# A hybrid decoder block on one core: expert gate and up weights loaded as two neighbouring rows per partition, and large tiles set at multiples of 128 bytes

## The chip, the core and the metric

The kernel runs on one core of one Trainium2 chip, as a single launch. The metric is the device time of one execution in microseconds (us). Three runs of the kernel before gave 1133.46, 1133.92 and 1135.08 us; their median is 1133.92 us.

The engines are called by the profile's names: PE (matrix multiply; PEld is its weight load), DVE (vector), ACT (scalar), POOL (GpSimd) and SP (here nearly only an issuer of DMAs). A name with a q at its end (SPq, ACTq) is the instruction queue of that engine.

## The reference

512 tokens of width 1024 go through one block: a mixer (retention, differential attention, gates and an output projection w_out) and a mixture of 32 experts. The change touches the second half and the vectors that feed it. All data are float32.

```
h  = rmsnorm(x, norm_ffn) * (1 + sc2) + sh2
gp = softmax(h @ w_router_group + b)          # 4 groups, the best one is taken
el = (h @ w_router_expert + b)                # 8 experts in a group, the best two are taken
y  = (silu(x_e @ w_exp_gate[e]) * (x_e @ w_exp_up[e])) @ w_exp_down[e]    # for each expert e
x  = x + g2 * sum of the two weighted y of each token
```

w_exp_gate and w_exp_up are 1024 x 512 for each expert, w_exp_down is 512 x 1024. Each of the three is 2 MB for one expert, so all 32 experts read 192 MB from memory.

## The kernel before

The trace has four stages: modulation vectors (0 to 95 us), projections, retention and attention (to about 590), w_out with the router for four chunks of 128 tokens (590 to 640), and the experts (640 to 1115), after which the result is normalised and written.

**Split matrices.** w_out is multiplied in high and low parts. A staging tile `wst` of 128 x 4 x 512 is loaded (L171). `split_kp` (L160) lets ACT copy half of it to `whi` (L163), and DVE subtract to get `wlo` (L164). The second column half of w_out has four such pairs; three go this way, the fourth (`hi4`, `lo4`, in the trace `ew`) through ACT at L1071 and POOL at L1072. All four pairs are needed before chunk 0 of the router stage can finish its product with w_out at L209, and the router chunks follow that.

**Router.** `wr` holds the router's weights, 128 partitions x 8 blocks x 36 columns; block k holds channels 128k to 128k+127. ACT's queue issues the two DMAs that fill it (L782, L783), then two for the biases `br`. `router_weights` (L801 to L805, DVE) folds norm and modulation into them. The token chunk `x1` is transposed in blocks of 128 channels (L870), and block k of `wr` meets block k of the transposed chunk in the logits (L877). `rows2` (L626) carries the modulation rows and norm_ffn; one transpose turns it into the columns `sh2` and `A2`, one column for each block of channels.

**Experts.** The work goes in 13 units of PE work of about 32 us each. A unit gathers the tokens of its experts by a product with a 0/1 matrix (L1000), transposes the gathered rows `xs` (L1031, eight transposes of 128 x 128), multiplies by gate and up (L1222), applies silu, multiplies by down (L1242) and adds the result back (L1269, L1275). The order of SP's instructions is the order of the code in `run_experts`: `load_in` issues eight loads for an expert (4 pairs of gate and up, L662), `load_down` four (L670). Each load is 512 KB into one of 36 weight slots of 4096 bytes per partition, used in turn (`wtile`, L643 to L650), so the slots hold three experts. A slot's next load waits until PE has used its last content. Loads for the first four units are of fixed experts, later ones are chosen by numbers that SP reads at run time (`chosen`).

A gate or up load takes rows 128(2kp) to 128(2kp)+255 of the matrix, two blocks, so that a partition gets two runs of 2048 bytes from places 256 KB apart. A down load gives each partition one run of 4096 bytes.

**Semaphores of DMAs.** DMAs issued by SP and ACT share eight completion semaphores, DMAHW0 to DMAHW7, given in turn in program order. An instruction that uses one again waits until the DMA before it on the same semaphore has landed.

**Pools.** SBUF tiles lie in pools that grow from the left or from the right end. Of the weight slots, those in `hp`, `mw1` and `mw4` are on the left and begin at multiples of 128 bytes; the 18 in `mw2` and `mw3` are on the right and begin 96 bytes past one, as do `wst`, `whi` and `wlo`. No code around the router or the experts sets an order by a planner: ACT, POOL and SP run in program order as built by the scheduler, and DVE and PE in an order written by hand for the router (L1073, L1085).

Of the kernel before, what the change touches and what calls it, by code (L numbers as in the profile page):

```python
# [7 lines left out]
F32 = mybir.dt.float32  # L8
# [5 lines left out]
ALU = mybir.AluOpType  # L14
# [32 lines left out]
ROTARY = (0, 0, 1, 1, 1)  # L47
ROWS_AT, COL_AT = 6, 12
LAMBDA_INIT = 0.8 - 0.6
TWO_PI = 2.0 * np.pi  # L50
# [50 lines left out]


class Rows:

# [15 lines left out]
def block_kernel(tc, a, out):  # L120
# [3 lines left out]
    def left(name, bufs=1):  # L124
        return open_pool(tc, name, bufs, side="left", reuse_waits="tile")

    def right(name, bufs=1):
        return open_pool(tc, name, bufs, side="right", reuse_waits="tile")

    w_in = a["w_in"][0]  # L130

    cp, cp_close = left("consts")
    hp, hp_close = left("hT")
    hla, hla_close = left("hla")
# [490 lines left out]

    rows2 = dp.tile([24, P], F32, name="rows2")  # L626
    nc.sync.dma_start(rows2[0:16, :], modrow[1:3, :].rearrange("s (k p) -> (s k) p", p=P))
    nc.sync.dma_start(rows2[16:24, :], a["norm_ffn"].rearrange("o (k p) -> (o k) p", p=P))
    sh2 = small("sh2", KD)
    A2 = small("A2", KD)  # L630
    run(out_steps)
    ps = pm.tile([P, S], F32, name="ps")
    pe.transpose(ps[:, 0:24], rows2, ident[0:24, 0:24])
    vec.tensor_copy(sh2, ps[:, 0:8])
    vec.tensor_scalar(A2, ps[:, 8:16], 1.0, None, op0=ALU.add)
    vec.tensor_mul(A2, A2, ps[:, 16:24])

# [17 lines left out]
    def load_in(srcs):  # L655

        ws = [{} for _ in srcs]
        for kp in range(KD // 2):
            for w, src in zip(ws, srcs):
                for name in ("w_exp_gate", "w_exp_up"):  # L660
                    w[name, kp] = wtile()
                    nc.sync.dma_start(w[name, kp], src(name)[:, 2 * kp:2 * kp + 2, :])  # L662
        return ws
# [9 lines left out]
    def fixed(e):  # L673
        return lambda name: a[name][0, e].rearrange("(k p) n -> p k n", p=P)

    def chosen(reg):
        return lambda name: a[name][0, bass.ds(reg, 1)].rearrange("e (k p) n -> p (e k) n", p=P)

# [84 lines left out]
    xp, xp_close = left("x1")  # L763
    gp, gp_close = left("gather")
    hh2, hh2_close = left("h2")
    rt, rt_close = right("router")
# [14 lines left out]
    nc.scalar.dma_start(g1b, modrow[0].partition_broadcast(P))  # L781
    nc.scalar.dma_start(wr[:, :, 0:4], a["w_router_group"][0].rearrange("(k p) n -> p k n", p=P))  # L782
    nc.scalar.dma_start(wr[:, :, 4:36], a["w_router_expert"][0].rearrange("(k p) n -> p k n", p=P))  # L783
    nc.scalar.dma_start(br[:, 0:4], a["b_router_group"][0].partition_broadcast(P))
# [48 lines left out]
    class Chunk:  # L833
# [30 lines left out]
        def turn(self, g):  # L864
            if g == 0:
                self.xT = rt.tile([P, KD, P], F32, name="x1T", bufs=2)
            ps = pm.tile([P, S], F32, name="ps")
            for q in range(4):
                k = 4 * g + q
                pe.transpose(ps[:, q * P:(q + 1) * P], x1[:, self.i, k * P:(k + 1) * P], ident)  # L870
            act.copy(self.xT[:, 4 * g:4 * g + 4, :], ps.rearrange("p (k t) -> p k t", k=4))
# [92 lines left out]
    class Gather:  # L964
# [60 lines left out]
        def turn(self, xT):  # L1025
            self.xT = xT
            for j in range(2):
                pt = self.pt() if j == 0 else self.pa()
                for q in range(4):
                    k = 4 * j + q  # L1030
                    pe.transpose(pt[:, q * P:(q + 1) * P], self.xs[:, k * P:(k + 1) * P], ident)  # L1031
                for q in range(4):
# [144 lines left out]
    mw3, mw3_close = right("mw3")  # L1177
    mk, mk_close = right("moe")

    places = slots(mw1, 5, 7) + slots(mw2, 10) + slots(mw3, 8) + slots(mw4, NMW4)  # L1180
# [344 lines left out]
    hp_close()  # L1525
    dram_close()
    cp_close()

# [23 lines left out]
```

## Time and profile before

| what | value |
|---|---|
| median of three runs | 1133.92 us |
| the profiled execution | 1135.46 us |
| its span, first to last instruction | 1133.7 us |
| mean granted TensorE clock | 0.989 |
| PE busy | 1071.7 us (95%) |
| PEld busy | 665.0 us (59%) |
| DVE busy | 622.2 us (55%) |
| ACT busy | 338.4 us (30%) |
| POOL busy | 79.0 us (7%) |
| read from memory | 280.88 MB |

The profiled execution took 1.5 us more than the median, of which 1.8 us lie outside the span. PE is busy in nearly every slice of the span, DMA engines are at 90% or more from about 620 us on, and both stay so until 1105 us; the page's busy shares do not tell which of the two sets the time of which stretch, so the queries below look at stretches, at the waits in them and at the rates of single stretches.

### The profile page before, as it was taken

The numbers are of one execution on the slowest core, as the hardware profiler recorded it, in microseconds if no ns is written. First come the engines' busy times: TensorE is split into PE (matmuls) and PEld (weight loads), VectorE is DVE, ScalarE is ACT, GpSimd is POOL, SyncE is SP. The second block draws the span as 40 slices with busy tenths as digits, with TensorE's granted clock in tenths as the row PEclk, the third lists the DMA queues.
The fourth block names the chain that finished last, engine by engine and source line by source line (L and its number), as shares of the span: only waits on it lengthen the run. The fifth ranks groups of instructions, "written<-read, shape, count | busy, mean of one in ns | idle before, by whom it ended". The sixth has DMA issues, their size and how long they took to land.

```text
span 1133.7 us, 15015 instructions
## 1 busy us (share of the span) xinstructions
PE 1071.7 (95%) x5178; PEld 665.0 (59%) x5178; DVE 622.2 (55%) x1443; ACT 338.4 (30%) x701; POOL 79.0 (7%) x106
## 2 busy tenths in 40 slices
PE   5999999999999999999999899999999999999885
PEld 3777778778788776788877444444432443234222
DVE  3468667644445765655775765755442553244244
ACT  4553233333343534444334211111111110111123
POOL 1031000000021111000013100000000000000001
PEclk9999999999999999999999999999999999999998
DMA  9945645622323221244286899999999999999994
GB/s 317 274 149 186 222 132 185 204 76 81 105 82 105 75 74 39 75 151 146 91 278 235 302 373 391 391 400 393 391 392 400 392 391 391 400 393 394 389 397 159
DMA packets 139889, 284.02 MB, mean 251 GB/s; under 512 B 10977, under 2 KB 34585, under 8 KB 139681
## 3 DMA queue, kind: packets, MB, share of 16 engines
q1 hardware_dynamic: 136656, 281.29, 68.6%
q10 hardware_dynamic: 3152, 1.73, 0.6%
q8 instruction: 42, 0.69, 0.3%
q14 instruction: 39, 0.31, 0.1%
HBM read 280.88 MB, written 2.11 MB: 250 GB/s over the span
## 4 chain that ended last, share of the span: by engine, by line
PE 67%; DMA 19%; DVE 7%; ACT 2%; issue 2%; POOL 1%; SPq 0%; ACTq 0%; DVEq 0%; POOLq 0%
PE pj L209 31%; PE gu L1222 12%; DMA ew<-in_w_exp_up_dram 9%; DMA ew<-in_w_exp_down_dram 5%; PE py L1242 5%; PE pa L1000 4%; PE pa L1269 4%; DMA wa<-in_w_ada_dram 3%; PE pj L391 2%; PE ps L485 2%; PE ps L695 1%; DMA wst<-in_w_in_dram 1%; DVE acc L462 1%; PE ps L391 1%; DVE qk L448 1%
## 5 line engine op out<-in xcount | busy, mean ns | idle before, releaser
L1222 PE MATMUL gu<-ew,xT 128*64 128x512 f32 (+1 forms) x1088 | 222.4, 601 | 12.6 <-DMA ew<-in_w_exp_gate_dram 8.4
L209 PE MATMUL pj<-ew,whi 128*128 128x512 f32 x512 | 168.2, 410 | 0.0
L164 DVE TENSOR_TENSOR wlo<-wst,whi 128x1024 fp32r<-128x1024 f32 x79 | 100.0, 1267 | 87.0 <-ACT whi L163 79.5
L209 PE MATMUL pj<-whi,ew 128*128 128x512 f32 x384 | 131.0, 409 | 2.8 <-DVE v L480 2.8
L1222 PEld LDWEIGHTS gu<-ew,xT 128*64 128x64 f32 (+1 forms) x1088 | 54.4, 123 | 133.7 <-issue 88.4
L1242 PE MATMUL py<-ew,hTm 128*64 128x512 f32 (+1 forms) x544 | 116.1, 599 | 6.9 <-DMA ew<-in_w_exp_down_dram 6.8
L163 ACT CAST whi<-wst 128x1024 fp32r<-128x1024 f32 x79 | 82.8, 1050 | 130.3 <-PE pj L209 122.1
L209 PEld LDWEIGHTS pj<-ew,whi 128*128 128x128 f32 x512 | 94.2, 190 | 23.6 <-issue 2.8
L209 PE MATMUL pj<-ew,wlo 128*128 128x512 f32 x256 | 101.8, 398 | 0.0
L209 PEld LDWEIGHTS pj<-whi,ew 128*128 128x128 f32 x384 | 73.6, 192 | 22.8 <-DVE v L480 3.2
L1275 DVE TENSOR_TENSOR x<-x,pa 128x512 f32<-128x512 f32 x96 | 59.5, 682 | 47.4 <-PE pa L1269 47.4
L1247 DVE SCALAR_TENSOR_TENSOR yt<-py,ws,g2b 64x512 f32<-64x512 f32 x52 | 39.0, 750 | 72.3 <-PE py L1242 71.7
L1242 PEld LDWEIGHTS py<-ew,hTm 128*64 128x64 f32 (+1 forms) x544 | 27.9, 123 | 84.1 <-issue 44.3
L209 PE MATMUL pj<-wlo,ew 128*128 128x512 f32 x192 | 76.9, 401 | 0.0
L1227 DVE TENSOR_TENSOR sg<-sg,gu 64x512 f32<-64x512 f32 x26 | 17.9, 690 | 97.1 <-ACT sg L1226 96.3
L209 PEld LDWEIGHTS pj<-ew,wlo 128*128 128x128 f32 x256 | 48.5, 189 | 11.7
L1269 PE MATMUL pa<-xs,ct 128*128 128x512 f32 x196 | 52.8, 409 | 0.1
L209 PE MATMUL pj<-xhi,whi 128*128 128x512 f32 x128 | 51.7, 404 | 0.0
L1269 PEld LDWEIGHTS pa<-xs,ct 128*128 128x128 f32 x196 | 35.0, 188 | 26.9 <-issue 12.4
L209 PE MATMUL pj<-xhi,wlo 128*128 128x512 f32 x128 | 50.7, 396 | 0.0
L209 PE MATMUL pj<-xlo,whi 128*128 128x512 f32 x128 | 50.7, 396 | 0.0
L1263 ACT CAST xs<-yt 128x512 fp32r<-128x512 f32 x25 | 15.5, 619 | 112.9 <-DVE yt L1247 68.1
(364 smaller groups left out, 1548.1 us busy)
## 6 DMA issues: line engine op xcount, KB each, us to landing
ew<-in_w_exp_gate_dram SPq DMA_DIRECT2D x128, 512.0 KB, 10.6
ew<-in_w_exp_up_dram SPq DMA_DIRECT2D x128, 512.0 KB, 10.7
ew<-in_w_exp_down_dram SPq DMA_DIRECT2D x128, 512.0 KB, 10.4
wa<-in_w_ada_dram SPq DMA_DIRECT2D x44, 512.0 KB, 4.8
wst<-in_w_in_dram SPq DMA_DIRECT2D x20, 1024.0 KB, 5.6
wst<-in_w_in_dram SPq DMA_DIRECT2D x16, 512.0 KB, 4.3
wst<-in_w_ret_o_dram SPq DMA_DIRECT2D x4, 1024.0 KB, 4.9
wst<-in_w_diff_o_dram SPq DMA_DIRECT2D x4, 1024.0 KB
```

The costliest lines, as they stand in the source:

```text
L163: act.copy(hi, src[:, off:off + 2, :])
L164: vec.tensor_sub(lo, src[:, off:off + 2, :], hi.bitcast(F32))
L209: pe.matmul(bank, l, r, start=(k == 0 and j == 0), stop=(k == KD - 1 and j == 2))
L391: pe.matmul(bank, w, (hhi, hhi, hlo)[m][:, k, :], start=(k == 0 and m == 0), stop=(k == KD - 1 and m == 2))
L485: pe.matmul(out, l[a_], r[b_], start=start and j == 0, stop=stop and j == 2)
L1000: pe.matmul(ps, self.G[:, i, :], hx[:, i, ns], start=(i == 0 and j == 0), stop=(i == NT - 1 and j == 1))
L1222: pe.matmul(self.gu[r:r + n, :], self.g.xT[:, k, c:c + n], w[name, k // 2][:, k % 2, :], start=(k == 0), stop=(k == KD - 1))
L1227: vec.tensor_mul(self.sg, self.sg, self.gu[64:P, :])
L1242: pe.matmul(py[r:r + n, :], self.hT[:, k, n * q:n * q + n], w[k][:, nh, :], start=(k == 0), stop=(k == 3))
L1247: vec.scalar_tensor_tensor(yt[r, ns], py[64 * nh:64 * nh + 64, :], self.g.w[r], g2b[r, ns], op0=ALU.mult, op1=ALU.mult)
L1269: pe.matmul(po, self.ct[:, i * P:(i + 1) * P], self.ys[nh][:, j, :], start=start and j == 0, stop=(j == 1))
L1275: vec.tensor_add(x1[:, i, ns], x1[:, i, ns], po)
```

## The change

**Pads.** A tile of 24 floats (96 bytes per partition) is taken first from the right end, and another of 8 floats in the pool `moe`. In the pools `gather` and `moe` the large tiles are taken once in a row ahead of the small ones. In the built program all large tiles then begin at multiples of 128 bytes, the 18 right-hand weight slots and `wst`, `whi` and `wlo` among them.

**Gate and up.** A load now takes rows 256q + 2p and 256q + 2p + 1 into partition p: two neighbouring rows, one run of 4096 bytes. The bytes, the slots and the number of loads stay. With that, block k = 2q + j of a matrix holds channels 256q + 2p + j instead of 128k + p.

**What has to match.** A new function `block(x, k)` reads these channels out of a row, that is every second float. It is used in the router's 32 transposes and in the 104 transposes of gathered rows. `rows2` becomes 12 rows of 256, turned by two transposes. `wr` is filled by eight DMAs on ACT's queue (for each of four q the group's and the expert's columns) in place of two; the number of small pieces, 1024 of 16 bytes and 1024 of 128 bytes, is the same.

```diff
--- before.py
+++ after.py
@@ -46,6 +46,8 @@
 START_STEPS = (1, 2, 2, 2, 1)
 ROTARY = (0, 0, 1, 1, 1)
 ROWS_AT, COL_AT = 6, 12
+
+TOP_PAD, MOE_PAD = 24, 8
 LAMBDA_INIT = 0.8 - 0.6
 TWO_PI = 2.0 * np.pi
 
@@ -100,6 +102,11 @@
     return parts
 
 
+def block(x, k):
+
+    return x.rearrange("s (q c j) -> s q j c", j=2, c=P)[:, k // 2, k % 2, :]
+
+
 class Rows:
 
 
@@ -130,6 +137,8 @@
     w_in = a["w_in"][0]
 
     cp, cp_close = left("consts")
+    top, top_close = right("top")
+    top.tile([P, TOP_PAD], F32, name="pad")
     hp, hp_close = left("hT")
     hla, hla_close = left("hla")
     rot, rot_close = left("rotary")
@@ -623,17 +632,20 @@
     mg = [hlb.tile([P, 2, KD, P], F32R, name=f"mg{i}") for i in range(NT)]
 
 
-    rows2 = dp.tile([24, P], F32, name="rows2")
-    nc.sync.dma_start(rows2[0:16, :], modrow[1:3, :].rearrange("s (k p) -> (s k) p", p=P))
-    nc.sync.dma_start(rows2[16:24, :], a["norm_ffn"].rearrange("o (k p) -> (o k) p", p=P))
+    rows2 = dp.tile([12, 2 * P], F32, name="rows2")
+    nc.sync.dma_start(rows2[0:8, :], modrow[1:3, :].rearrange("s (q c) -> (s q) c", c=2 * P))
+    nc.sync.dma_start(rows2[8:12, :], a["norm_ffn"].rearrange("o (q c) -> (o q) c", c=2 * P))
     sh2 = small("sh2", KD)
     A2 = small("A2", KD)
     run(out_steps)
     ps = pm.tile([P, S], F32, name="ps")
-    pe.transpose(ps[:, 0:24], rows2, ident[0:24, 0:24])
-    vec.tensor_copy(sh2, ps[:, 0:8])
-    vec.tensor_scalar(A2, ps[:, 8:16], 1.0, None, op0=ALU.add)
-    vec.tensor_mul(A2, A2, ps[:, 16:24])
+    for j in range(2):
+        pe.transpose(ps[:, 12 * j:12 * j + 12], block(rows2, j), ident[0:12, 0:12])
+    cols2 = ps[:, 0:24].rearrange("p (j s q) -> p j s q", j=2, s=3)
+    sh2v, A2v = [t.rearrange("p (q j) -> p j q", j=2) for t in (sh2, A2)]
+    vec.tensor_copy(sh2v, cols2[:, :, 0, :])
+    vec.tensor_scalar(A2v, cols2[:, :, 1, :], 1.0, None, op0=ALU.add)
+    vec.tensor_mul(A2v, A2v, cols2[:, :, 2, :])
 
 
     def slots(pool_, *places):
@@ -659,7 +671,7 @@
             for w, src in zip(ws, srcs):
                 for name in ("w_exp_gate", "w_exp_up"):
                     w[name, kp] = wtile()
-                    nc.sync.dma_start(w[name, kp], src(name)[:, 2 * kp:2 * kp + 2, :])
+                    nc.sync.dma_start(w[name, kp].rearrange("p j n -> p (j n)"), src(name)[:, kp, :])
         return ws
 
     def load_down(srcs):
@@ -671,10 +683,13 @@
         return ws
 
     def fixed(e):
-        return lambda name: a[name][0, e].rearrange("(k p) n -> p k n", p=P)
+        return lambda name: (a[name][0, e].rearrange("(k p) n -> p k n", p=P) if name == "w_exp_down" else
+                             a[name][0, e].rearrange("(q p j) n -> p q (j n)", p=P, j=2))
 
     def chosen(reg):
-        return lambda name: a[name][0, bass.ds(reg, 1)].rearrange("e (k p) n -> p (e k) n", p=P)
+        at = bass.ds(reg, 1)
+        return lambda name: (a[name][0, at].rearrange("e (k p) n -> p (e k) n", p=P) if name == "w_exp_down" else
+                             a[name][0, at].rearrange("e (q p j) n -> p (e q) (j n)", p=P, j=2))
 
 
     dohi = hla.tile([P, KD, S], F32R, name="xhi")
@@ -762,6 +777,8 @@
 
     xp, xp_close = left("x1")
     gp, gp_close = left("gather")
+    for name, cols in (("G", NT * P), ("xs", D), ("xT", D), ("oht", P)):
+        gp.tile([P, cols], F32, name=name, bufs=1)
     hh2, hh2_close = left("h2")
     rt, rt_close = right("router")
     mw1, mw1_close = left("mw1")
@@ -779,8 +796,11 @@
     wr = rt.tile([P, KD, 36], F32, name="wr")
     br = rt.tile([P, 36], F32, name="br")
     nc.scalar.dma_start(g1b, modrow[0].partition_broadcast(P))
-    nc.scalar.dma_start(wr[:, :, 0:4], a["w_router_group"][0].rearrange("(k p) n -> p k n", p=P))
-    nc.scalar.dma_start(wr[:, :, 4:36], a["w_router_expert"][0].rearrange("(k p) n -> p k n", p=P))
+    wrv = wr.rearrange("p (q j) n -> p q j n", j=2)
+    for q in range(KD // 2):
+        rs = slice(2 * P * q, 2 * P * q + 2 * P)
+        nc.scalar.dma_start(wrv[:, q, :, 0:4], a["w_router_group"][0, rs].rearrange("(p j) n -> p j n", j=2))
+        nc.scalar.dma_start(wrv[:, q, :, 4:36], a["w_router_expert"][0, rs].rearrange("(p j) n -> p j n", j=2))
     nc.scalar.dma_start(br[:, 0:4], a["b_router_group"][0].partition_broadcast(P))
     nc.scalar.dma_start(br[:, 4:36], a["b_router_expert"][0].partition_broadcast(P))
     nc.scalar.dma_start(iota, a["cst"][:, C_IOTA:C_IOTA + 512])
@@ -867,7 +887,7 @@
             ps = pm.tile([P, S], F32, name="ps")
             for q in range(4):
                 k = 4 * g + q
-                pe.transpose(ps[:, q * P:(q + 1) * P], x1[:, self.i, k * P:(k + 1) * P], ident)
+                pe.transpose(ps[:, q * P:(q + 1) * P], block(x1[:, self.i, :], k), ident)
             act.copy(self.xT[:, 4 * g:4 * g + 4, :], ps.rearrange("p (k t) -> p k t", k=4))
 
         def logits(self, g):
@@ -1028,7 +1048,7 @@
                 pt = self.pt() if j == 0 else self.pa()
                 for q in range(4):
                     k = 4 * j + q
-                    pe.transpose(pt[:, q * P:(q + 1) * P], self.xs[:, k * P:(k + 1) * P], ident)
+                    pe.transpose(pt[:, q * P:(q + 1) * P], block(self.xs, k), ident)
                 for q in range(4):
                     k = 4 * j + q
                     if j:
@@ -1176,6 +1196,9 @@
     mw2, mw2_close = right("mw2")
     mw3, mw3_close = right("mw3")
     mk, mk_close = right("moe")
+    for name, cols in (("ct", 512), ("sg", 512), ("yt", D), ("hTm", 256), ("tab", P)):
+        mk.tile([P, cols], F32, name=name, bufs=1)
+    mk.tile([P, MOE_PAD], F32, name="pad")
 
     places = slots(mw1, 5, 7) + slots(mw2, 10) + slots(mw3, 8) + slots(mw4, NMW4)
     tiles = {(p, j): p.tile([P, 2, 512], F32, name=f"ew{j}") for p, j in places}
@@ -1524,6 +1547,7 @@
     xp_close()
     hp_close()
     dram_close()
+    top_close()
     cp_close()
```

On ACT's queue, behind the casts of the attention output (`mg`), stand the router's loads and the casts of w_out. `g1b` is the gate vector, `wr` and `br` the router's weights and biases, `ew5` is `hi4`. Before:

```order
L781 DMA g1b_4733<-modrow_81 128x1024 [waits DVE_49]
L782 DMA wr_4736<-in_w_router_group_dram 128x8x4 [waits DMAHW2_49]
L783 DMA wr_4736<-in_w_router_expert_dram 128x8x32 [waits DMAHW3_49]
L784 DMA br_4737<-in_b_router_group_dram 128x4 [waits DMAHW4_49]
L785 DMA br_4737<-in_b_router_expert_dram 128x32 [waits DMAHW5_49]
L163 CAST whi_4900<-wst_4892 128x1024 [waits DMAHW1_49,PE_49]
L1071 CAST ew5_4721<-wst_4894 128x1024 [waits DMAHW1_49]
L163 CAST whi_4911<-wst_4892 128x1024 [waits PE_49]
L163 CAST whi_4921<-wst_4894 128x1024 [waits DVE_49,PE_49]
```

In the changed kernel, from the third of the eight `wr` loads on:

```order
L802 DMA wr_4745<-in_w_router_group_dram 128x2x4 [waits DMAHW4_49]
L803 DMA wr_4745<-in_w_router_expert_dram 128x2x32 [waits DMAHW5_49]
L802 DMA wr_4745<-in_w_router_group_dram 128x2x4 [waits DMAHW6_49]
L803 DMA wr_4745<-in_w_router_expert_dram 128x2x32 [waits DMAHW7_49]
L802 DMA wr_4745<-in_w_router_group_dram 128x2x4 [waits DMAHW0_49]
L803 DMA wr_4745<-in_w_router_expert_dram 128x2x32 [waits DMAHW1_49]
L804 DMA br_4746<-in_b_router_group_dram 128x4 [waits DMAHW2_49]
L805 DMA br_4746<-in_b_router_expert_dram 128x32 [waits DMAHW3_49]
L1091 CAST ew5_4730<-wst_4909 128x1024
L172 CAST whi_4915<-wst_4907 128x1024 [waits PE_49]
L172 CAST whi_4926<-wst_4907 128x1024 [waits PE_49]
L172 CAST whi_4936<-wst_4909 128x1024 [waits DVE_49,PE_49]
```

There are six more DMAs ahead of the casts, the last of them waits for DMAHW1, and the cast of `ew5` has moved from behind the first cast of `whi` to the front of it. What DMAHW0 and DMAHW1 stand for at that place: DMAHW0 was last given to the load of `g1b`, DMAHW1 to the last load of w_out, which the cast of `ew5` reads.

On SP's queue the order is the same. The piece shows the end of the first expert's gate and up loads. Before:

```order
L662 DMA ew4_4727<-in_w_exp_gate_dram 128x2x512 [waits DMAHW2_49,Pool_49]
L662 DMA ew0_5468<-in_w_exp_up_dram 128x2x512 [waits DMAHW3_49,DVE_49,Pool_49]
L662 DMA ew1_5469<-in_w_exp_gate_dram 128x2x512 [waits DMAHW4_49]
L662 DMA ew2_5470<-in_w_exp_up_dram 128x2x512 [waits DMAHW5_49]
L670 DMA ew3_5471<-in_w_exp_down_dram 128x1024 [waits DMAHW6_49]
```

In the changed kernel:

```order
L674 DMA ew4_4736<-in_w_exp_gate_dram 128x1024 [waits DMAHW0_49,Pool_49]
L674 DMA ew0_5489<-in_w_exp_up_dram 128x1024 [waits DMAHW1_49,DVE_49,Pool_49]
L674 DMA ew1_5490<-in_w_exp_gate_dram 128x1024 [waits DMAHW2_49]
L674 DMA ew2_5491<-in_w_exp_up_dram 128x1024 [waits DMAHW3_49]
L682 DMA ew3_5492<-in_w_exp_down_dram 128x1024 [waits DMAHW4_49]
```

The gate and up loads have the form of the down loads, 128 x 1024, and the semaphores are shifted by six, so that two of them are now shared with late `wr` loads.

## Rows read from the trace of the kernel before

**Rows 1.** The chain that ended last, by engine, from the page.

```profile
PE 67%; DMA 19%; DVE 7%; ACT 2%; issue 2%; POOL 1%; SPq 0%; ACTq 0%; DVEq 0%; POOLq 0%
```

**Rows 2.** Windows: length, busy us (PE, PEld, DVE, ACT, POOL), clock, DMA share, GB/s.

```profile
700.00:800.00 100.00, 100.00 (x562) 42.57 (x560) 54.87 (x138) 16.29 (x34) 0.00 (x0) 1.00 1.04 394
...
900.00:1000.00 100.00, 94.92 (x479) 34.65 (x476) 41.20 (x95) 14.24 (x30) 0.00 (x0) 1.00 1.04 393
1000.00:1100.00 100.00, 91.07 (x422) 34.30 (x420) 41.61 (x86) 16.71 (x33) 0.00 (x0) 1.00 1.04 393
```

**Rows 3.** SP's waits in 640:700, 700:760, 760:830: total us, times, longest.

```profile
SPq L662 <- PE gu L1222: 23.2, 15, 5.3
...
SPq L662 <- PE gu L1222: 7.7, 6, 2.9
...
SPq L662 <- PE gu L1222: 1.2, 3, 0.4
```

**Rows 4.** PE's longest sum of waits in 960:1105, same columns.

```profile
PE gu L1222 <- DMA ew<-in_w_exp_gate_dram: 6.7, 7, 1.7
```

**Rows 5.** Windows of POOL, for the last two columns: gate/up packets only.

```profile
836.00:848.00 12.00, 0.00 (x0) 1.00 1.05 387
1075.00:1087.00 12.00, 0.00 (x0) 1.00 1.05 387
...
913.00:923.00 10.00, 0.00 (x0) 1.00 1.05 386
...
1048.00:1060.00 12.00, 0.00 (x0) 1.00 1.05 384
```

**Rows 6.** The same view: w_exp_down packets only.

```profile
762.00:772.00 10.00, 0.00 (x0) 1.00 1.02 408
1092.00:1105.00 13.00, 0.00 (x0) 1.00 1.02 403
```

**Rows 7.** DMA view: SP's queue in 836:848 and 1092:1105; gate issues from 740.

```profile
q1 hardware_dynamic: 2401, 4.64, 105.2%
...
q1 hardware_dynamic: 1451, 5.24, 101.7%
...
ew<-in_w_exp_gate_dram SPq DMA_DIRECT2D x88, 512.0 KB, 10.7
```

**Rows 8.** Chain by time (start, us, what): w_out's last load, a down load.

```profile
578.62 7.19 DMA wst<-in_w_out_dram
...
851.08 10.11 DMA ew<-in_w_exp_down_dram
```

**Rows 9.** Timeline of ACT: start, us, instruction, [idle before <-releaser].

```profile
578.31 0.60 ACTq L783 DMA_DIRECT2D wr<-in_w_router_expert_dram  x1
...
582.15 1.05 ACT L163 CAST whi<-wst 128x1024 fp32r<-128x1024 f32 x1 [5.94 <-DMA wr<-in_w_router_group_dram]
585.84 1.05 ACT L1071 CAST ew<-wst 128x1024 fp32r<-128x1024 f32 x1 [2.63 <-DMA wst<-in_w_out_dram]
```

**Rows 10.** Timelines of DVE and (last row) PE: w_out's low parts.

```profile
587.87 2.64 DVE L164 TENSOR_TENSOR wlo<-wst,whi 128x1024 fp32r<-128x1024 f32 x1 [1.31 <-ACT whi L163]
590.44 0.68 DVE L826 SCALAR_TENSOR_TENSOR tm<-pj,g1b 128x512 f32<-128x512 f32 x1
...
593.25 1.22 DVE L164 TENSOR_TENSOR wlo<-wst,whi 128x1024 fp32r<-128x1024 f32 x1
...
594.52 0.50 PE L209 MATMUL pj<-wlo,mg 128*128 128x512 f32 x1 [1.85 <-DVE wlo L164]
```

**Rows 11.** Windows, columns of Rows 2: where PE has gaps.

```profile
632.00:636.00 4.00, 2.27 (x16) 1.41 (x14) 3.46 (x20) 0.00 (x0) 0.62 (x1) 0.86 1.03 402
636.00:640.00 4.00, 3.60 (x16) 2.34 (x17) 1.21 (x5) 1.78 (x5) 0.00 (x0) 0.71 0.64 234
```

**Rows 12.** L870's weight loads (ns: least/median/most); POOL's split in 586:592.

```profile
L870 PEld LDWEIGHTS ps<-cst,x x32: 137/140/144, 591.6 to 628.3; 128*128 128x128 f32 x32
...
587.04 2.40 POOL L1072 TENSOR_TENSOR ew<-wst,ew 128x1024 fp32r<-128x1024 f32 x1
```

## The prediction, made before the changed kernel was run

> **What bounds the kernel now.** I read the chain of work that ended last first: PE has 67% of it and DMA 19% [rows 1], so two things set the end, in different stretches. The windows tell which is where [rows 2]: from 700 to 800 us PE has no idle time; from 900 to 1000 and from 1000 to 1100 it idles 5.1 and 8.9 us, while DMA moves 393 GB/s at a share above 1 throughout. The waits of SP's queue tell when it changes [rows 3]: a gate or up load waits for PE to give back a slot for 23.2 us in 640 to 700, 7.7 us in 700 to 760, and 1.2 us in 760 to 830. From then on loads wait only for earlier loads, and PE waits for them, most for gate [rows 4]. So up to some 740 us the slots, that is PE, set when loads start; from there to 1105 us the loads set the end, with 88 gate, as many up and 96 down loads [rows 7]. A microsecond saved in the load rate after 740 us is a microsecond off the end; a microsecond lost by PE before it moves the whole of what follows.
>
> Within the load-bound stretch I looked at pieces in which packets of one kind alone land. Gate and up, runs of 2048 bytes: 387, 387, 386 and 384 GB/s [rows 5]. Down, runs of 4096 bytes: 408 and 403 GB/s [rows 6]. The first two rows of [rows 5] are loads into left slots, at multiples of 128 bytes, the last two into right slots, 96 bytes past one: the address is worth 0.5% at the most, the length of the run about 5%.
>
> **What the change brings: longer runs.** Every gate and up load takes the form of a down load. One is 524288 bytes. Weighting the rows by their lengths gives 386.0 GB/s or 1.358 us a load now, and 405.2 GB/s or 1.294 us as down does. 176 loads after 740 us times 0.064 us are **11.3 us**. The nearest rows bound it: 387 against 403 gives 9.5 us, 384 against 408 gives 14.1. Another reading goes higher: the packets' own time per MB is 1.052 x 12 / 4.64 = 2.72 us in the gate and up window and 1.017 x 13 / 5.24 = 2.52 in the down window [rows 7], 7.3% less, and of 176 x 1.358 = 239 us that is 17.4 us. I keep the rate, since shares above 1 show that packets' times overlap. PE could follow: it idles 14.0 us in the last two windows alone. The 52 gate and up loads from 640 to 740 us wait for slots and gain nothing.
>
> **The pads** alone are worth 0.5% of the gate and up loads into right slots, about half of 239 us: 0.6 us at most, taken as nothing. No price is given to the loads' issue on SP either, since SP waits for landings there.
>
> **What it costs: ACT's queue before the router.** In the order of ACT the casts of w_out stand behind all router loads. Now the eighth of them waits on DMAHW1 for the last w_out load, issued at 578.62 and landed 7.19 us later, at 585.81 [rows 8]. Before, only the cast of `ew5` waited for it (585.84), and the first `whi` was cast at 582.15 [rows 9]. Queued behind the waiting issue are two bias loads, the cast of `ew5` (now first) and three casts of `whi`; DVE waits for the casts and PE for DVE. Step by step: three issues at up to 0.60 us, taken as 1.6 together, to 587.4; `ew5` 1.05 to 588.5; `whi` 1.05 to 589.5. DVE follows with the first `wlo`, 1.22 us, to 590.7, two steps of 0.68 for the residual to 592.1, the second `wlo` in 1.22 to 2.64 us (2.64 is what it took beside POOL's 2.40 us split [rows 10, 12]) to 593.3 or 594.7. From the next L826 to the start of the third `wlo` before were 593.25 - 590.44 = 2.8 us, which gives 596.1 or 597.5, and its 1.22 us 597.3 or 598.8. Before, this end was 594.47, and PE, which had waited for it, went on at 594.52 [rows 10]. The delay is 2.9 to 4.3 us; I take **3.6 us**. From there PE, the router's chunks and the first experts follow in one chain, so it counts in full.
>
> PE then has gaps through most of 589 to 598 us. Where it had gaps before, 628 to 640 us, the granted clock fell to 0.86 and 0.71 in the two windows [rows 11]: (0.14 + 0.29) x 4 = 1.7 us lost. A like drop is to be bounded by 0 and 1.7 us; since these gaps are the longer, I take **1.7 us**.
>
> SP's sixth gate or up load now waits for the eighth `wr` load's landing. That one leaves at 585.8 us and SP's came at 594.5 us, so some 8 us cover it.
>
> **What it costs: strided transposes.** Weight loads of the router's transposes take 140 ns [rows 12]. No row shows one that reads every second float. If that doubled them and nothing hid it, the 32 of L870, the 8 of the first gather and the 24 of L1031 from 640 to 740 us, which lie on PE's path, would cost 64 x 0.14 = 9.0 us; below nothing it can't be, since no byte less is read. Later ones fall into PE's idle time. I take 0, because PEld runs beside PE's matmuls (43 us of it beside 100 us of PE [rows 2]). The second transpose of `rows2` and its DVE views add some 0.1 us.
>
> **Sum.** 1135.46 - 11.3 + 3.6 + 1.7 + 0.1 = 1129.6 us for an execution like the profiled one. That one lay 1.5 us above the median of the runs, so the forecast of the median is **1128.0 us**, 0.5% faster. About 0.2%, 2.3 us, is what a measurement of this kernel can tell from no change: same means 1131.6 to 1136.2.
>
> **Rivals.**
> *Slower: the rate does not follow the run length.* Mechanism: the down rows reach 405 GB/s because of something else, and what limits gate and up is the memory or the fabric as a whole. For it speaks that the rate sits at 393 or 394 in every long window [rows 2], like a ceiling; against it, that down alone moves 5% more in the same kernel, at a lower share. Then the gain is 0 and the delays stay: 1135.46 + 5.4 - 1.5 = 1139.4. It decides below a gain of 3.1 us, that is if the gate and up loads reach less than 391 GB/s. [...]
>
> [...]
>
> *Faster: the stall is hidden.* The `wr` issue waits less, or ACT's casts were not what PE waited for (before it waited for the third `wlo`, which also hangs on DVE's own queue): 1135.46 - 11.3 + 0.1 - 1.5 = 1122.8.
>
> *Strided transposes cost their bound:* 1128.0 + 9.0 = 1137.0.
>
> *The packets' time is the measure:* 17.4 us gained, 1128.0 - 6.1 = 1121.9, if PE can follow.
>
> **How the numbers follow.** Forecast 0.50 (1125 to 1132 by its own bounds; of it 0.06 falls within 0.2%), rate does not follow 0.13, half the gain 0.08, stall hidden 0.15, strided transposes 0.08 (0.05 of it slower, 0.03 same), packets' time 0.06. Faster: 0.44 + 0.15 + 0.06 = 0.65. Same: 0.06 + 0.08 + 0.03 = 0.17. Slower: 0.13 + 0.05 = 0.18. The range goes from 1121.5, just under the two faster rivals, to 1137.0, the strided bound; it leaves out the case of no gain and a sum of two good ones, together under 0.2.
>
> **What would show it.** Right: stretches of gate and up at 403 to 408 GB/s like down, long windows from 740 us on at about 405 instead of 393; the first cast of `whi` at about 588.5 instead of 582.15 with a wait for the w_out load or an issue ahead of it; PE's wait for the third `wlo` ending at 597 to 599 us; a fall of the granted clock near 600 us; weight loads of L870's and L1031's successors at 140 ns. Wrong: gate and up still under 391 GB/s; PE back on the path to the end, with SP's loads waiting for slots far past 760 us, so that faster loads find no slot; transposes that take longer than before.

## The result and the profile after

The changed kernel takes **1116.14 us** (median; 1116.05 to 1116.26), the kernel before in the same comparison 1135.08 us. The ratio is 0.984, with a 95% interval from 0.981 to 0.986. Forecast were 1128.0 us and a range down to 1121.5: the direction was right, the gain of 18.9 us is more than three times the forecast one (5.9 us), and the time lies outside the range. One of the changed kernel's five executions, the profiled one, took 2594.25 us at a granted clock of 1.00, with the matmuls of the projections at 826 to 858 ns instead of some 400; it is left out here, and why it was slow is open.

The trace shown below as that of the changed kernel is therefore of a later execution (a_five), of 1117.24 us with a span of 1115.4 us. First the windows, with the columns of [rows 2]:

```profile
700.00:800.00 100.00, 100.00 (x560) 42.98 (x558) 55.59 (x139) 16.67 (x34) 0.00 (x0) 1.00 1.02 405
800.00:900.00 100.00, 98.20 (x520) 41.17 (x518) 48.77 (x116) 15.48 (x32) 0.00 (x0) 1.00 1.03 409
900.00:1000.00 100.00, 96.86 (x486) 39.06 (x484) 43.35 (x101) 13.60 (x27) 0.00 (x0) 1.00 1.03 409
```

The load stage moves 409 GB/s where it moved 393 [rows 2], and PE idles 3.1 us from 900 to 1000 where it idled 5.1. Loads still set the end. SP's waits for PE's slots are as in [rows 3], 7.7 us in 700:760 (first row) and 1.4 us in 760:830 (last row), where most waits are already for landings (second row):

```profile
SPq L674 <- PE gu L1245: 7.7, 4, 4.9
...
SPq L674 <- DMA ew<-in_w_exp_down_dram: 11.2, 15, 1.3
...
SPq L674 <- PE gu L1245: 1.4, 5, 0.4
```

The stall on ACT's queue is where it was forecast. These rows are of SP's, ACT's and DVE's timelines; beside [rows 8 to 10] the order of the casts has changed and they come together, after the eighth `wr` load:

```profile
568.64 0.38 SPq L180 DMA_DIRECT2D wst<-in_w_out_dram  x1
...
572.65 0.62 ACTq L802 DMA_DIRECT2D wr<-in_w_router_group_dram  x1
576.16 0.55 ACTq L803 DMA_DIRECT2D wr<-in_w_router_expert_dram  x1
...
577.89 1.05 ACT L1091 CAST ew<-wst 128x1024 fp32r<-128x1024 f32 x1 [11.65 <-DMA wr<-in_w_router_group_dram]
578.84 2.93 ACT L172 CAST whi<-wst 128x1024 fp32r<-128x1024 f32 x3
...
587.68 1.22 DVE L173 TENSOR_TENSOR wlo<-wst,whi 128x1024 fp32r<-128x1024 f32 x1
```

ACT's queue has nothing between 573.27 and 576.16 us. The eighth `wr` load, which shares its semaphore with w_out's load, leaves 7.5 us after that load's issue; before, w_out's load had landed 7.19 us after its issue [rows 8]. (What stands behind an arrow is the profile's inference, here another `wr` load.) From the issue of w_out's load to the first cast of `whi` it is 10.2 us, as forecast (588.5 - 578.62 = 9.9). To the start of the third `wlo` it is 19.04 us; before, 593.25 - 578.62 = 14.63 us [rows 8, 10]. The delay is 4.4 us. The granted clock then falls in two windows:

```profile
580.00:584.00 4.00, 1.92 (x5) 1.31 (x6) 3.96 (x4) 1.77 (x2) 1.38 (x1) 0.84 0.73 278
584.00:588.00 4.00, 3.64 (x13) 2.47 (x12) 3.93 (x8) 0.49 (x2) 0.00 (x0) 0.73 0.62 251
```

The strided transposes do show in their weight loads (in ns: least, median, most; the row of before is in [rows 12]):

```profile
L890 PEld LDWEIGHTS ps<-cst,x x32: 194/207/217, 586.5 to 623.1; 128*128 128x128 f32 x32
L890 PE MATMUL ps<-cst,x x32: 270/283/386, 586.8 to 623.3; 128*128 128x128 f32 x32
```

What the prediction had not looked for stands in the groups of the projections (95 to 560 us). Matmuls of two groups there, line, names, shapes, count, busy us and mean ns of one, of the kernel before (L209) and of the changed kernel (L218):

```profile
L209 PE MATMUL pj<-xhi,whi 128*128 128x512 f32 x118 | 47.8, 405 | 0.0
L209 PE MATMUL pj<-xhi,wlo 128*128 128x512 f32 x118 | 46.7, 396 | 0.0
```

```profile
L218 PE MATMUL pj<-xhi,whi 128*128 128x512 f32 x128 | 50.9, 398 | 0.0
L218 PE MATMUL pj<-xhi,wlo 128*128 128x512 f32 x128 | 49.9, 390 | 0.0
```

The counts differ because the window cuts the two kernels at different places. The second name is that of the weights. The same matmul has become 6 to 7 ns shorter in a stage with over 1100 that have `whi` or `wlo` as weights, in which no load of an expert and no router runs. No edit but the pads touches it.

### The profile page after: what moved, and what is told of

It reads as the page before. It is cut to its first block, busy times and chain, and to the rows that moved or that the text cites. A ratio compares the mean times of both kernels' runs of the same rounds, so it can differ in the third digit from the quotient of the medians.

```text
span 2592.5 us, 15021 instructions
## 1 busy us (share of the span) xinstructions
PE 2570.7 (99%) x5179; PEld 1214.5 (47%) x5179; DVE 631.0 (24%) x1443; ACT 341.4 (13%) x701; POOL 76.5 (3%) x106
## 4 chain that ended last, share of the span: by engine, by line
PE 99%; DMA 0%; DVE 0%; ACT 0%; ACTq 0%; issue 0%; POOLq 0%; POOL 0%; DVEq 0%
PE pj L218 44%; PE gu L1245 19%; PE py L1265 10%; PE pa L1292 5%; PE pa L1020 5%; PE pj L400 3%; PE ps L494 3%; PE ps L710 2%; PE ps L400 1%; PE ps L545 1%; PE ps L565 1%; PE ps L383 1%; PE ps L897 1%; PE pt L1255 1%; PE pt L1051 1%; PE pa L1051 1%
## 5 line engine op out<-in xcount | busy, mean ns | idle before, releaser
L1245 PE MATMUL gu<-ew,xT 128*64 128x512 f32 (+1 forms) x1088 | 507.5, 1406 | 0.0
L218 PE MATMUL pj<-ew,whi 128*128 128x512 f32 x512 | 379.9, 858 | 0.0
L218 PE MATMUL pj<-whi,ew 128*128 128x512 f32 x384 | 287.6, 848 | 0.0
L1265 PE MATMUL py<-ew,hTm 128*64 128x512 f32 (+1 forms) x544 | 250.5, 1416 | 0.0
L218 PEld LDWEIGHTS pj<-ew,whi 128*128 128x128 f32 x512 | 179.2, 358 | 117.6 <-issue 115.5
L218 PE MATMUL pj<-ew,wlo 128*128 128x512 f32 x256 | 211.4, 826 | 0.0
L218 PEld LDWEIGHTS pj<-whi,ew 128*128 128x128 f32 x384 | 135.7, 353 | 92.1 <-issue 89.9
L218 PE MATMUL pj<-wlo,ew 128*128 128x512 f32 x192 | 159.0, 828 | 0.0
L1292 PE MATMUL pa<-xs,ct 128*128 128x512 f32 x196 | 121.7, 811 | 0.0
L218 PEld LDWEIGHTS pj<-ew,wlo 128*128 128x128 f32 x256 | 90.3, 353 | 61.4 <-issue 60.9
L218 PE MATMUL pj<-xhi,whi 128*128 128x512 f32 x128 | 108.5, 848 | 0.0
L218 PE MATMUL pj<-xlo,whi 128*128 128x512 f32 x128 | 106.0, 828 | 0.0
L218 PE MATMUL pj<-xhi,wlo 128*128 128x512 f32 x128 | 105.9, 827 | 0.0
L218 PEld LDWEIGHTS pj<-wlo,ew 128*128 128x128 f32 x192 | 69.3, 361 | 44.4 <-issue 44.2
```

The source lines that it names most:

```text
L218: pe.matmul(bank, l, r, start=(k == 0 and j == 0), stop=(k == KD - 1 and j == 2))
L1245: pe.matmul(self.gu[r:r + n, :], self.g.xT[:, k, c:c + n], w[name, k // 2][:, k % 2, :], start=(k == 0), stop=(k == KD - 1))
L1265: pe.matmul(py[r:r + n, :], self.hT[:, k, n * q:n * q + n], w[k][:, nh, :], start=(k == 0), stop=(k == 3))
L1292: pe.matmul(po, self.ct[:, i * P:(i + 1) * P], self.ys[nh][:, j, :], start=start and j == 0, stop=(j == 1))
```

## Where the time went: stages

DVE runs the same instructions in the same order in all these kernels, so the starts of eight of them cut every trace into the same nine stages. The cuts are, in the kernel before: L474 at 160.46 us, L698 at 366.79, L164 at 509.73, L506 at 575.40, L827 at 597.35, L952 at 643.55, L1247 at 773.14, and L1444, the last instruction but a few, at 1125.95. A is the stage up to the first cut. The other rows are worked out from the experiments' traces below, one execution each.

| kernel | A | B | C | D | E (w_out) | F (router) | G | H (loads) | I |
|---|---|---|---|---|---|---|---|---|---|
| before | 160.5 | 206.3 | 142.9 | 65.7 | 21.9 | 46.2 | 129.6 | 352.8 | 7.7 |
| pads alone (b_pads) | 158.6 | 202.5 | 141.5 | 64.5 | 22.0 | 46.7 | 129.6 | 352.9 | 7.8 |
| eight wr loads alone (f_wr8) | 158.4 | 206.5 | 141.4 | 65.7 | 25.7 | 47.7 | 129.6 | 353.2 | 8.0 |
| long runs, no stall (g_loads) | 159.8 | 206.6 | 142.9 | 65.7 | 21.9 | 46.5 | 130.1 | 338.2 | 8.0 |
| changed kernel (a_five) | 157.9 | 203.0 | 140.0 | 64.5 | 26.4 | 47.1 | 130.1 | 338.1 | 8.3 |
| changed, no stall (d_five) | 159.5 | 201.6 | 141.5 | 64.5 | 21.3 | 47.1 | 130.1 | 337.9 | 7.9 |

Stages B, D, E, G and H go by the edits: B and D shorten with the pads, by 3.4 to 4.7 and 1.2 us; E is 3.7 to 5 us longer with the eight `wr` loads ahead of the casts; G, in which PE sets the pace (busy 131.4 of the 133 us from 640 to 773 us before), is 0.5 us longer with the strided transposes; H is 14.6 us shorter with the long runs. A, C and F differ by up to 3 us between these executions, and F and A show no order by the edits. B has 588 matmuls with `whi` or `wlo` as weights and PE idles for 1.0 of its 206.3 us before, so that 3.8 us in b_pads are 6.5 ns for each; D has 216 and gains about 5.5 ns for each.

One cause of this spread can be read. PE has a gap near 400 us in each of the four traces shown here, and at it the granted clock falls in three of them and not in the fourth. Windows of the gap, first of before, then of the changed kernel:

```profile
396.00:400.00 4.00, 1.89 (x11) 1.39 (x10) 3.55 (x6) 0.83 (x2) 2.70 (x2) 0.92 0.00 0
400.00:404.00 4.00, 4.00 (x15) 3.19 (x15) 2.57 (x9) 0.95 (x3) 0.00 (x0) 0.65 0.00 0
```

```profile
388.00:392.00 4.00, 2.25 (x10) 1.50 (x8) 3.56 (x5) 2.27 (x5) 2.71 (x3) 1.00 0.00 0
392.00:396.00 4.00, 3.54 (x21) 2.93 (x22) 4.00 (x11) 0.96 (x2) 1.03 (x1) 1.00 0.00 0
```

By an estimate from these clocks before lost (0.08 + 0.35) x 4 = 1.7 us there, this execution of the changed kernel none.

The same gap in the pads alone and in the long runs without stall:

```profile
392.00:396.00 4.00, 3.32 (x13) 2.67 (x14) 3.95 (x9) 0.37 (x1) 1.25 (x2) 0.67 0.00 0
396.00:400.00 4.00, 4.00 (x22) 3.52 (x21) 2.05 (x7) 2.35 (x6) 0.00 (x0) 0.90 0.00 0
```

```profile
396.00:400.00 4.00, 1.89 (x9) 1.68 (x9) 3.56 (x6) 0.46 (x2) 2.69 (x2) 0.79 0.00 0
400.00:404.00 4.00, 4.00 (x18) 3.20 (x17) 2.58 (x11) 1.23 (x4) 0.00 (x0) 0.78 0.00 0
```

Each lost 1.7 us too by the same estimate. With these losses taken off, stage C has an order after all: 142.9 - 1.7 = 141.2 us before, 141.4 in f_wr8 (no loss) and 141.2 in g_loads, against 141.5 - 1.7 = 139.8 in b_pads and 140.0 in a_five (no loss). In all seven kept traces of kernels whose `whi` and `wlo` are off it is 140.8 to 141.4 us, in nine of the others 139.6 to 140.0. The pads gain 1.4 us in C as well, which the clock hides in the table.

## The experiments

Theory 1 was the prediction's: longer runs make the gain, pads nothing, the stall takes some back. The rival was that the tiles' addresses make a good part of the gain. Times are medians; each is compared with the kernel before timed beside it.

**The changed kernel again, and the parts.**

> The changed kernel once more, for a profile at the usual matmul rate. Both theories: about 1116 us, 18 to 19 us under the kernel before. Theory 1 (longer runs): gate and up stretches move 403 GB/s or more, and loads set the end to 1105 us less the gain. Rival (pads): stretches into the slots that were 96 bytes off gain more than the left ones. If the stall on ACT's queue is real, the first cast of whi starts at about 588.5 us and PE's wait for the third wlo ends at 597 to 599 us.

Measured: 1116.11 us against 1132.81.

The pads alone are the hunks with `TOP_PAD`, `MOE_PAD`, `top`, and the tiles taken in a row in `gather` and `moe`, put into the kernel before.

> The kernel before with the pads alone (top pad, moe pad, large tiles taken in a row); loads as before. Theory 1 (longer runs make the gain): 0 to -0.6 us, within 0.2% of before. Rival (the address of the tiles makes a good part of it): -5 us or more, 1129 or less.

Measured: 1127.47 us, a ratio of 0.995 (0.993 to 0.996): **5.3 us** faster. The prediction's price of 0.6 us is wrong. The load stage has not moved (H 352.9 against 352.8), so it is not the loads that gain. The matmuls have:

```profile
L213 PE MATMUL pj<-xhi,whi 128*128 128x512 f32 x128 | 50.9, 398 | 0.0
L213 PE MATMUL pj<-xhi,wlo 128*128 128x512 f32 x128 | 49.9, 390 | 0.0
```

The new loads, transposes and `wr` loads without those hunks:

> The changed kernel without the pads: the new loads, transposes and wr loads with the tiles where they were. Theory 1: within 1 us of the changed kernel, about 1116 to 1117. Rival: what the pads give is missing, 1121 or more. If pads and long runs only work together, both this and the pads alone fall short and their sum misses 5 us or more.

Measured: 1124.04 us, 0.991 (0.989 to 0.993), 8.8 us faster than before and 7.9 us slower than the changed kernel. Both parts count.

**The stall.** In the changed kernel the `wr` and, with them, the `br` loads are moved behind the first cast of `whi`:

```diff
-    for q in range(KD // 2):
-        rs = slice(2 * P * q, 2 * P * q + 2 * P)
-        nc.scalar.dma_start(wrv[:, q, :, 0:4], ...)
-        nc.scalar.dma_start(wrv[:, q, :, 4:36], ...)
...
         kps = [split_kp(sts[0], 0)]
+        for q in range(KD // 2):
+            rs = slice(2 * P * q, 2 * P * q + 2 * P)
+            nc.scalar.dma_start(wrv[:, q, :, 0:4], ...)
+            nc.scalar.dma_start(wrv[:, q, :, 4:36], ...)
```

> The changed kernel with the router's weights and biases issued on ACT behind the first cast of whi, so that this cast waits for nothing new. If the stall on ACT's queue costs what the prediction took (3.6 us and 1.7 us of clock), this is 3 to 5 us faster than the changed kernel, 1111 to 1113. If the stall is hidden or absent: within 1 us of it.

Measured: 1113.08 us against 1116.11, 3.0 us faster. Both kernels once more, timed beside each other:

> The changed kernel in five rounds, to be compared with the next. 1116 us.

> The changed kernel with the router's loads behind the first cast of whi, in five rounds. If the stall costs 3 us as in the first comparison: 1113 us. If the traces' 4 to 7 us are right: 1110 to 1112.

Measured: 1117.56 and 1114.10 us against 1133.87 of before; the stall costs 3.5 us by the medians, 5.0 by stages E and F of these two traces and 4.3 by those of a_again and d_wrlate. ACT's timeline without the stall has the casts apart again: a first `whi` at 569.96 us, the cast of `ew` 6.5 us after the issue of w_out's load (570.28 us), the next `whi` 1.7 us later:

```profile
574.04 0.62 ACTq L1091 DMA_DIRECT2D wr<-in_w_router_group_dram  x1
576.79 1.05 ACT L1084 CAST ew<-wst 128x1024 fp32r<-128x1024 f32 x1 [5.77 <-DMA wr<-in_w_router_expert_dram]
576.79 0.55 ACTq L1092 DMA_DIRECT2D wr<-in_w_router_expert_dram  x1
...
578.52 1.05 ACT L172 CAST whi<-wst 128x1024 fp32r<-128x1024 f32 x1 [0.68 <-PE pj L218]
```

Then the stall by itself, put into the kernel before with the channels as they were:

```diff
-    nc.scalar.dma_start(wr[:, :, 0:4], ...)
-    nc.scalar.dma_start(wr[:, :, 4:36], ...)
+    for q in range(KD // 2):
+        rs, ks = slice(2 * P * q, 2 * P * q + 2 * P), slice(2 * q, 2 * q + 2)
+        nc.scalar.dma_start(wr[:, ks, 0:4], a["w_router_group"][0, rs].rearrange("(k p) n -> p k n", p=P))
+        nc.scalar.dma_start(wr[:, ks, 4:36], a["w_router_expert"][0, rs].rearrange("(k p) n -> p k n", p=P))
```

> The kernel before with one edit: the router's weights come by eight DMAs on ACT's queue in place of two (same channels, same small pieces), so that the eighth waits for the last w_out load and the casts stand as in the changed kernel. If the stall is a cost of its own: slower than before by 3 to 6 us, PE's wait for the third wlo near 598 us. If it is hidden: within 1 us of before.

Measured: 1138.93 us against 1133.87, 1.005 (1.003 to 1.007): **5.1 us** slower. The timelines of SP, ACT and DVE, and the windows:

```profile
575.23 0.38 SPq L171 DMA_DIRECT2D wst<-in_w_out_dram  x1
...
583.29 0.37 ACTq L785 DMA_DIRECT2D wr<-in_w_router_expert_dram  x1
...
594.50 1.22 DVE L164 TENSOR_TENSOR wlo<-wst,whi 128x1024 fp32r<-128x1024 f32 x1
```

```profile
588.00:592.00 4.00, 2.30 (x7) 1.39 (x8) 3.96 (x5) 0.60 (x1) 0.20 (x1) 0.79 0.97 363
592.00:596.00 4.00, 3.00 (x11) 2.22 (x12) 3.93 (x8) 1.37 (x4) 0.00 (x0) 0.78 0.45 172
```

19.27 us from the issue of w_out's load to the third `wlo`, 4.6 more than before, and a clock of 0.79 and 0.78: (0.21 + 0.22) x 4 = 1.7 us, an estimate like the prediction's. The delay is the prediction's mechanism in all its steps. The fall of the clock is not tied to it, though. In c_loads, the changed kernel without the pads, which has the stall, PE has the gaps and the clock does not fall (first fence), and E is only 3.3 us longer than in g_loads; in d_wrlate, which has no stall, it falls in the same place (second fence):

```profile
588.00:592.00 4.00, 1.98 (x8) 1.05 (x6) 3.97 (x4) 1.63 (x2) 1.26 (x1) 1.00 0.73 286
592.00:596.00 4.00, 2.19 (x11) 1.61 (x10) 3.93 (x8) 0.62 (x2) 0.00 (x0) 1.00 0.59 240
```

```profile
584.00:588.00 4.00, 2.88 (x9) 2.32 (x10) 3.93 (x5) 1.39 (x4) 1.29 (x1) 0.78 1.01 401
588.00:592.00 4.00, 4.00 (x17) 3.27 (x16) 2.12 (x4) 0.72 (x2) 0.00 (x0) 0.80 0.89 329
```

**What the pads act on.** Theory 2: a matmul of L209 is longer when its weight tile, `whi` or `wlo`, does not begin at a multiple of 128 bytes. Four kernels, each the kernel before with pads of another size or place. e_top24 has the first hunk alone, with 24 floats; e_top8 and e_top16 have 8 and 16 there; e_wst96 has both hunks:

```diff
+    top, top_close = right("top")
+    top.tile([P, 24], F32, name="pad")
...
     wp, wp_close = right("wts")
+    for _ in range(2):
+        wp.tile([P, 4, 512], F32, name="wst", bufs=2)
+    wp.tile([P, 8], F32, name="pad")
```

> The kernel before with the 96-byte pad at the right end alone; the pools gather and moe as before. Theory 2 (a weight tile off a multiple of 128 bytes makes each matmul of L209 longer, so the pads gain in the projections): the same as all pads, 5 to 8 us under before, and the matmuls xhi x wlo at 390 ns instead of 396. Rival (the pools gather and moe matter): about 0, as before.

> The same with a pad of 32 bytes: wst, whi, wlo and the right-hand slots begin 64 bytes past a multiple of 128. If multiples of 64 are enough, as the 96-byte pad: matmuls xhi x wlo at 390 ns, 5 to 8 us under before. If only multiples of 128 count: matmuls at 396 ns, no gain.

> The same with a pad of 64 bytes: these tiles begin 32 bytes past a multiple of 128. By both readings of theory 2 no gain, matmuls at 396 ns. If it gains as much as the 96-byte pad, the address modulo 128 is not the cause.

> The 96-byte pad at the right end and a pad of 32 bytes between wst and whi: whi and wlo, which PE reads, begin at multiples of 128 bytes; the staging tiles wst, which DMA writes and ACT and DVE read, and the right-hand tiles of the retention stage begin 96 past, as before. Theory 2 (PE's reading of the operand): the gain of the pads is there, matmuls xhi x wlo at 390 ns. Rival (DMA, ACT and DVE at wst disturb PE): no gain, 396 ns.

| kernel | whi, wlo begin past a multiple of 128 by | wst by | median, us | ratio to before (1133.22 us) |
|---|---|---|---|---|
| e_top24 | 0 | 0 | 1128.52 | 0.996 (0.994 to 0.998) |
| e_top8 | 64 | 64 | 1132.54 | 0.999 (0.998 to 1.000) |
| e_top16 | 32 | 32 | 1132.90 | 1.000 (0.998 to 1.001) |
| e_wst96 | 0 | 96 | 1128.58 | 0.996 (0.994 to 0.997) |

The same group of matmuls, one fence for each kernel, in the table's order:

```profile
L211 PE MATMUL pj<-xhi,wlo 128*128 128x512 f32 x128 | 49.9, 390 | 0.0
```

```profile
L211 PE MATMUL pj<-xhi,wlo 128*128 128x512 f32 x124 | 49.0, 395 | 0.0
```

```profile
L211 PE MATMUL pj<-xhi,wlo 128*128 128x512 f32 x121 | 47.9, 396 | 0.0
```

```profile
L214 PE MATMUL pj<-xhi,wlo 128*128 128x512 f32 x128 | 49.9, 390 | 0.0
```

Where `whi` and `wlo` lie at multiples of 128 it is 390 ns, else 395 or 396; 64 is not enough. `wst`, written by DMA and read by ACT and DVE, lay 96 past without a loss that shows (1128.58 us against 1128.52), and the top pad alone does it; the pads in `gather` and `moe` bring nothing that can be seen (4.7 us under before without them, 5.3 with them, intervals of some 2 us). One rival is left by these runs: ACT and DVE write `whi` and `wlo` at the same addresses, and their writing could disturb PE. The traces speak against it. The matmuls at full clock with `whi` or `wlo` as weights (the few over 450 ns left out) took 395.9 ns before and 389.6 in e_top24 while ACT, DVE and POOL all stood still, and 396.1 and 390.4 while one of these tiles was being written. So the 6 ns go with the place at which the weights of a matmul begin, not with the writing.

For the moving operand, the first name, no gain is shown. These are groups of before and of the changed kernel in which `whi` moves:

```profile
L209 PE MATMUL pj<-whi,ew 128*128 128x512 f32 x335 | 115.5, 411 | 2.8 <-DVE v L480 2.8
```

```profile
L218 PE MATMUL pj<-whi,ew 128*128 128x512 f32 x335 | 112.9, 403 | 3.5 <-DVE v L489 3.4
```

But the 411 ns are a mean over stretches in which the granted clock of before was 0.66 (105 to 110 and 135 to 140 us). In stage B, at a clock of 1.00, the same group took 402 ns before, and `pj<-wlo,ew` 393, against 403 and 395 over the whole window in the changed kernel. In `pj<-whi,mg` of before `whi` moved from 96 bytes past at a median of 389 ns.

**The long runs alone.** Without pads and without the stall:

> The changed kernel without pads and without the stall: new loads, transposes, and the router's loads behind the first cast of whi. If the longer runs gain what the traces show between 640 us and the end (14 us) and the strided transposes cost under 1 us, 13 to 14 us under before, near 1120. If the gain is the 11.3 us of the prediction: near 1122.

Measured: 1121.56 us against 1133.87, 0.990 (0.987 to 0.992), 12.3 us faster, between the two readings and nearer to the prediction's 11.3.

What stayed open was the sum: -5.3 for the pads, -12.3 for the long runs and +5.1 for the stall make -12.5, and the changed kernel is 16 to 17 us under before where it was timed again. Three kernels timed beside one another, to see whether pads and long runs add up:

> Pads alone, once more beside the next two in the same call, for a table of two by two without the stall (before, pads, loads, both). Alone the pads gave 4.6 to 5.3 us. If pads and long runs add up, this minus before equals both minus loads, within 1.5 us.

> New loads without pads and without the stall. 12 us under before by the first run. If the stages' times in the traces (14.5 us from the first experts to the end, 0.5 us given back by the transposes) are right, 13 to 14 us.

> New loads and pads without the stall. If the two add up: 5 us under the one before. If the pads are worth more beside faster loads: 7 us or more under it, as across the earlier calls.

Measured: before 1133.19, pads 1127.45, long runs 1121.59, both 1113.92 us. Pads give 5.7 us alone and 7.7 beside the long runs, which by its number is the second reading. The difference of 2 us came out here and between the first runs (5.3 alone, 7.9 from c_loads to the changed kernel), but each of these medians has an interval of about 2 us, and no stage of the traces shows it: B, D, G and H of the kernel with both are those of the parts. The stages that the edits govern sum to -5.2 (pads, B and D, mean of the table's three kernels with pads) - 14.6 + 0.5 + 0.2 (long runs, H, G and I) = -19.1, and with the pads' 1.4 in C to -20.5; g_both gained 19.3. The medians of the pads alone (4.6 to 5.7, against 6.6 of stages) and of the long runs alone (11.6 and 12.3, against 13.9) fall short of their stages. That the executions lose different amounts by the clock, as in C, is shown; that this makes the whole difference is not.

The version without the stall is 1113 to 1114 us in three comparisons, faster than the kernel before (0.983, 0.981 to 0.985) and, by 3.0 and 3.5 us, than the changed kernel.

## Why the prediction was wrong, point by point

**Longer runs, 11.3 us.** Mechanism right, size a little low. 393 GB/s became 409, and stage H lost 14.6 us, just past the upper bound of 14.1. The term was mis-sized because the windows taken for down, 408 and 403, were only 10 and 13 us long and the lower one was the last stretch of the loads; with 4096-byte runs only, long windows hold 409. Medians give 11.6 to 12.3 us for it with the transposes' cost inside.

**The pads, taken as nothing.** This is the step that failed: "The pads alone are worth 0.5% of the gate and up loads into right slots". The rows behind it stand, and H does not change with the pads. But they speak only for the loads (H 352.9 us against 352.8). (The lowest right row, 384, is 0.8% under the left ones, not 0.5% at the most; that would be 1 us, as little.) The pads also move `wst`, `whi` and `wlo`, which the section on the change names among their tiles, and `whi` and `wlo` feed nearly every matmul of the projections. All `whi` and `wlo` were off before, but the trace had the same matmul with both operands on the left, at multiples of 128 bytes, in the stage ahead of the projections:

```profile
L391 PE MATMUL ps<-ew,xhi 128*128 128x512 f32 x32 | 9.7, 390 | 0.0
```

Beside the 396 ns of `pj<-xhi,wlo` it hints at 6 ns for each matmul of L209 with `whi` or `wlo` as weights; the page of before has 512 + 256 + 3 x 128 = 1152 of them, an estimate of 6.9 us. (This group takes 390 ns in the changed kernel too.) The pads gave 4.6 to 5.7 us alone by the medians, 6.6 by the stages B, C and D. As a term of 5 us they would have brought the forecast to some 1123.

**The stall, 3.6 us, and the clock, 1.7.** The delay is right in place and order, and nearly in size: 4.4 us in the changed kernel's trace, against a bound of 4.3. The clock's share there is (0.16 + 0.27) x 4 = 1.7 us, an estimate. With its clock the stall cost 5.1 us by itself in the kernel before, against 5.3 forecast; in the changed kernel its removal gained 3.0 and 3.5 us by the medians, 2 us less than forecast. The clock's term was partly luck: with the stall the clock fell here in a_five (0.84 and 0.73), a_again (0.77 and 0.80) and f_wr8 (0.79 and 0.78) but not in c_loads (1.00 and 1.00), and without the stall it fell in d_wrlate (0.78 and 0.80).

**SP's shifted semaphores.** As forecast, no cost: in a_again SP's sixth load leaves at 592.38 us, when the third `wlo` is done (592.32), 20.4 us after w_out's load where it was 15.9 before; the eighth `wr` load left 12.8 us earlier (579.57).

**Strided transposes, 0 of at most 9.0 us.** Nearly right in time, though the sign named for it, weight loads at 140 ns, did not come. The weight load takes 207 ns where it took 140 [rows 12], but runs beside PE's matmuls: of the 67 ns the matmul shows 11 (medians of 272 ns at L870 and 283 at L890), and stage G grew by 0.5 us. Why a load that reads every second float takes half as long again, no run here shows.

**The rivals.** That the rate does not follow the run length is refuted by 409 GB/s. Half the gain, given a chance of 0.08, did not come, and no run shows a term of that size: the rate rose 4%, from 393 to 409 GB/s, in stretches that were two thirds gate and up, and H lost 14.6 us. The stall was not hidden (4.4 us later at the third `wlo`). The reading by packets' time (17.4 us) was too high by some 3 us.

**What remains.** With the pads' 5.2 and the loads' 14.6 us in their places the prediction's own sum is 1128.0 - 5.2 - 3.3 = 1119.5 us, plus 0.5 for the transposes. The kernel lies 3 to 4 us under this. The pads' gain in C is 1.4 us of it, and the stall's price, 3.0 to 3.5 us in place of 5.3, some 2 us. What is then left is under 1 us, less than the interval of any of these medians, so that the near agreement is partly luck.

## What to carry to other kernels

When a change moves tiles, list every engine that reads or writes each of them, and price each; here the row that cleared the loads said nothing of the matmul, where the pads gave 4.6 to 5.7 us. Look at the start addresses of the tiles that matmuls take as weights, and try multiples of 128 bytes: here a pad of 96 bytes per partition brought such a matmul from 396 to 390 ns. When the granted clock falls in some executions, as near 400 us in three of four traces here (some 1.7 us each, an estimate), take its loss off a stage before comparing it. And when one DMA is cut into several, count the semaphores: here six added ones made ACT's queue wait for the last load of w_out ahead of casts that had not waited for it, which cost 5.1 us in f_wr8.

## What the runs showed of the hardware

- A 128 x 128 x 512 matmul of the split parts (type fp32r in the rows of their casts) took 390 ns (mean, as modelled) with both operands at multiples of 128 bytes, and 395 or 396 ns with the weights 32, 64 or 96 bytes past. With the moving operand 96 bytes past no loss showed (389 ns, median of `pj<-whi,mg` before). The matmuls of the experts, where the slot moves, showed none either (601 ns for L1222 before, on slots of both kinds, 600 for its successor in g_both; G 129.6 us with and without the pads).
- Loads with 4096 bytes per partition in a run went at 409 GB/s over windows of 100 us, with 2048 bytes at 384 to 387 over windows of 10 and 12 us [rows 5].
- A weight load of 128 x 128 float32 took 140 ns (median, L870 before), and 207 ns when it read every second float (L890, a_five); the matmul beside it 272 and 283 ns.
- After a gap of about 2 us in 4 the granted clock fell to 0.65 in one execution (before, 396:404) and not at all in another (changed kernel, 388:396).
